# A list scheduler that books VectorE and GpSimd around each other's SBUF reads

## The chip, the cores and the metric

The kernel runs on one core of one Trainium2 chip. The metric is the device time of one execution in microseconds (us), the median of several runs. Before the change it is 1306.06 us, the median of 3 runs that lay between 1305.51 and 1308.34 us.

## What is computed

The reference is one residual block in float32 on 1024 tokens of width 1024. All of it is computed by the kernel:

```
h    = rms_norm(x, norm_w) * (1 + scale(c)) + shift(c)
proj = h @ W_in               # q, k, v, z of mixer A; q, k, v, z of mixer B; two gates; beta, decay
A    : causal conv + SiLU on q, k, v; l2 norm of q, k; gated delta rule, 8 heads of 128
y_A  = (headwise rms_norm(A) * silu(z_A)) @ P_A
B    : causal window attention, 12 heads of 64, in 3 groups with dilations 1, 4, 16
y_B  = (o_B * softmax over the groups' log denominators * silu(z_B)) @ P_B
x    = x + gate(c) * ((sigmoid(g_A) * y_A + sigmoid(g_B) * y_B) @ W_o)
out  = rms_norm(x, final_norm_w)
```

## The kernel before, in words

**The products.** Activations lie transposed, as 8 tiles of 128 features by 1024 tokens. A float32 product is made of three TensorE products of rounded halves (`hi*hi`, `hi*lo`, `lo*hi`), each 128 by 512 at most. There are 4548 such products (with the projections' names `pj<-big,wh` and `pj<-wh,big` for most of them), and they are the bulk of TensorE's work. ScalarE rounds each weight tile to its `hi` half and GpSimd subtracts to get the `lo` half (`w_split`, L579; tiles `wr` in, `wh` out). The late projections are computed two at a time with Strassen's scheme (`pair`, L674): `w_combine` (L609) forms sums of weight blocks on GpSimd and VectorE (`sums`, L637; tile `ss`), and `pair_out` (L711) adds the seven products up on VectorE out of PSUM into tiles `mid`; a PSUM tile `pj` comes free when its last addition has read it.

**The small chains.** Beside the projections run many chains of small steps that go from TensorE to VectorE or ScalarE and back. `conv` (L855) filters a projection with three VectorE instructions. `n_stream` and `q_stream` (L1217, L1340) multiply a head's k with k and with q and scale the result. `inv_stream` (L1243) inverts 32 by 32 triangles for four heads with 62 VectorE instructions in a row (`mid<-big` and `big<-big,mid`), first for heads 0 to 3 (`inv0`), then for 4 to 7 (`inv1`). `merge_stream` (L1271) assembles each head's inverse by small products with evacuations between them, `rec_stream` (L1430) runs a head's 8 chunks of the delta rule, three products one after the other per chunk. `attn_unit` (L1531) is one piece of attention, `combine` (L1636) the weights of the three groups (tile `fga`). Between these, `part` (L821) rounds stored sums of h (named T1 to T4): it is issued as soon as its load is, so its ScalarE copy `big<-mid` can stand in ScalarE's queue before the load has landed.

**The planner.** The order of all engines is made by a list scheduler in the kernel's own Python code. Every chain is a generator (`Stream`), with a priority. `Sched.run` (L240) lets the chain of best priority go whose next step is due by the planner's own clock of TensorE, `clk["pe"]`; the big projections (`projections`, priority 99) fill what is left. Each instruction that is issued passes through `Sched.book` (L137), which adds a length to the clock of its engine and so settles when the chain is due again. The lengths are a table of formulas in ns: n elements per partition on VectorE cost n/0.96 + 150, a GpSimd `tensor_tensor` costs 2.2 n + 400. An engine's queue runs strictly in the order so made; on the chip nothing is reordered. So where a step takes longer than booked, TensorE reaches the step that needs it early, and stands.

Names in the profile: `L110` is the wrapper that issues nearly every instruction, so groups are told apart by tiles: `big` 128x1024 work tiles, `mid` 128x512, `pj` and `sb` PSUM tiles, `sq` 128x128, `TT` and `Xb` the inverses, `dnw` a norm weight.

Of the kernel before, what the change touches and what calls it, by code (L numbers as in the profile page):

```python
# [34 lines left out]
LO_POOL = ("A11", "S3")  # L35
WORKERS = 2
NMID = 6
BLK1 = "k1 k3 q0 q1"
NW = 8

# [4 lines left out]
def _free(ap):  # L45
    n = 1
    for s in list(ap.shape)[1:]:
        n *= s
    return n


class Event:
# [64 lines left out]
class Sched:  # L117


    def __init__(self, nc):  # L120
        self.clk = dict(pe=600.0, act=600.0, dve=600.0, pool=600.0, dma=600.0)
        self.streams = []
        self.cur = None
        self.pe = Engine(self, nc.tensor, "pe")
        self.act = Engine(self, nc.scalar, "act")
        self.dve = Engine(self, nc.vector, "dve")
        self.pool = Engine(self, nc.gpsimd, "pool")
        self.sp = Engine(self, nc.sync, "dma")
        self.table = None

    def now(self):
        return self.clk["pe"]
# [3 lines left out]

    def book(self, e, op, out, a, k):  # L137
        n = _free(a[1] if op == "tensor_reduce" else out)
        done = self.cur.done
        others = max([t for q, t in done.items() if q != e], default=0.0)  # L140
        start = max(self.clk[e], self.clk["pe"], others)
        if e == "pe":
            start = self.clk["pe"]
            if op == "transpose":
                c = 109
            else:
                r = k.get("rhs", a[2] if len(a) > 2 else None)
                if r.dtype == F32R:
                    c = n / 2.4 + 13.4
                elif r.shape[0] <= 64:  # L150
                    c = 30 if out.shape[0] == 32 else 60 if out.shape[0] == 64 else n / 1.1
                else:
                    c = n / 0.6 + 9 if n > 8 else 60
            end = start + c
            self.clk["pe"] = end
            hop = 190
        elif e == "dma":
            b = n * 4 * out.shape[0] * (2 if out.shape[-1] < P else 1)
            end = max(self.clk[e] + max(470, b / 360), max(self.clk["pe"], others) + 1500 + b / 360)
            self.clk[e] = end  # L160
            hop = 950
        else:
            if e == "act":
                c = n / 1.2 + (385 if "accum_out" in k else 195)
                if not isinstance(k.get("bias", 0.0), float) and "accum_out" not in k:
                    c += 160
                f = TABLE.get(k.get("func", a[2] if len(a) > 2 else None))
                if f and f != self.table:
                    self.table = f
                    c += 1280  # L170
            elif e == "dve":
                c = n / 0.96 + 150
                if op == "tensor_scalar":
                    c = n / 1.92 + 215
                elif op == "scalar_tensor_tensor" and n > 8:
                    c += 60
                elif op == "reciprocal":
                    c = n * 6.2 + 70
            else:
                c = n * 2.2 + 400 if op == "tensor_tensor" else n * 1.27  # L180
                if k.get("op") == OP.pow:
                    c = n * 165 + 300
                elif n == 8 * P and k.get("op") == OP.mult:
                    c = 1900
            end = start + c
            self.clk[e] = end
            hop = 130
        done[e] = end + hop
        self.cur.last = max(self.cur.last, end + hop)
# [79 lines left out]
def hybrid_block_kernel(ctx: ExitStack, tc: tile.TileContext, x, c, norm_w, ada_w, ada_b, w_tiles, w_vb0, w_vb1,  # L269
# [3 lines left out]
    pe, act, dve, pool, sp = S.pe, S.act, S.dve, S.pool, S.sp  # L273
# [305 lines left out]
    def w_split():  # L579
# [15 lines left out]
        for u in units[FIRST:]:  # L595
            if hasattr(u, "srcs"):
                yield from w_combine(u)
                continue
            yield u.raw_ev
            u.hi = yield from wh.get(F32R, shape=[P, u.n])  # L600
            u.lo = yield from wh.get(F32R, shape=[P, u.n])
            act.activation(u.hi, u.raw, AF.Copy)
            yield
            pool.tensor_tensor(u.lo, u.raw, u.hi.bitcast(F32), op=OP.subtract)
            wr.put()
            S.set(u.ev)
            yield S.now()

    def w_combine(u):  # L609
# [26 lines left out]

        def sums():  # L637
            yield u.raw_ev[1]
            pool.tensor_tensor(s1, a21, a22, op=OP.add)
            dve.tensor_tensor(s2, s1, a11, op=OP.subtract)  # L640
            S.set(ev_s2)
            yield ev_s2
            pool.tensor_tensor(a21, a11, a21, op=OP.subtract)
            S.set(ev_s3)
            yield u.ev["A12"]
            pool.tensor_tensor(a11, a12, s2, op=OP.subtract)
            S.set(ev_s4)

        ss = yield from spare.get()
        s2, s1 = ss[:, 0:half], ss[:, half:2 * half]  # L650
        ev_s2, ev_s3, ev_s4 = Event(), Event(), Event()
        yield lambda: u.raws
        a11, a12 = u.raws[0][:, 0:half], u.raws[0][:, half:]
# [1395 lines left out]
```

## Time and profile before

| what | us |
|---|---|
| median of 3 runs | 1306.06 |
| the profiled execution's own time | 1307.42 |
| its span, first to last instruction | 1305.7 |
| PE (TensorE) busy | 1228.0 |
| DVE (VectorE) busy | 825.0 |
| ACT (ScalarE) busy | 565.7 |
| POOL (GpSimd) busy | 484.1 |

The mean granted TensorE clock is 0.977 of full speed. In the chain of waits and in the instruction rows, the square brackets hold the idle time just before an instruction and what ended it. A row of the table by stages gives, for a stretch of time, the busy time of each engine, the granted clock and the DMA share.

### The profile page before, as it was taken

The page shows a single profiled execution, that of the slowest core. Times are in us where ns is not written, and L with a number is a line of the kernel's source. Part 1 is how long each engine was busy: PE and PEld are TensorE (multiplying, and loading weights), DVE is VectorE, ACT ScalarE, POOL GpSimd, SP SyncE. Part 2 cuts the span into 40 slices and gives each one's busy share as a digit, 9 for nine tenths or more (in the row PEclk, how much of TensorE's full clock was granted, in tenths as well). Part 3 has the DMA queues.
Part 4 walks back from the last instruction along what each step waited for, and adds up shares of the span by engine and source line. Part 5 has one row for each costly group of instructions (what it writes and reads, how often), then busy time and mean ns, then how long its engine had stood idle before and what let it go on. Part 6 is the DMA issues. An engine that isn't in the chain of part 4 may idle for free. (4 is left out here: it accounts for less than half of the span.)

```text
span 1305.7 us, 19690 instructions
## 1 busy us (share of the span) xinstructions
PE 1228.0 (94%) x7111; PEld 1012.7 (78%) x7111; DVE 825.0 (63%) x1477; ACT 565.7 (43%) x1176; POOL 484.1 (37%) x274
## 2 busy tenths in 40 slices
PE   5799999997977999999899999999989999999997
PEld 3598888876967888877688778877777788888886
DVE  6667798999675655546655865466465557365433
ACT  5547544553242435455533436773542341122211
POOL 4632834642031543432424343245234422123400
PEclk9899999998978999999899999999999999999999
DMA  9464566872854465547785576457445498343422
GB/s 357 145 203 155 153 202 200 260 230 71 253 173 154 134 200 160 149 122 223 247 255 181 167 214 188 127 163 245 144 119 161 130 313 279 120 155 124 144 97 82
DMA packets 166739, 234.99 MB, mean 180 GB/s; under 512 B 42953, under 2 KB 107633, under 8 KB 166642
## 3 DMA queue, kind: packets, MB, share of 16 engines
q1 hardware_dynamic: 166498, 233.47, 56.3%
q8 instruction: 56, 0.92, 0.3%
q14 instruction: 41, 0.34, 0.1%
q10 hardware_dynamic: 144, 0.26, 0.1%
HBM read 154.86 MB, written 78.83 MB: 179 GB/s over the span
## 5 line engine op out<-in xcount | busy, mean ns | idle before, releaser
L110 PE MATMUL pj<-big,wh 128*128 128x512 f32 x3468 | 869.2, 401 | 17.3 <-POOL big L110 8.1
L110 PEld LDWEIGHTS pj<-big,wh 128*128 128x128 f32 x3468 | 636.8, 190 | 156.2 <-POOL big L110 10.1
L110 POOL TENSOR_TENSOR wh<-wr,wh 128x1024 fp32r<-128x1024 f32 (+4 forms) x92 | 215.6, 2344 | 427.0 <-ACT wh L110 357.9
L110 ACT ACTIVATE wh<-wr 128x1024 fp32r<-128x1024 f32 (+4 forms) x119 | 109.9, 924 | 186.9 <-PE pj L110 109.8
L110 DVE TENSOR_TENSOR mid<-mid,pj 128x512 f32<-128x512 f32 x150 | 106.3, 722 | 87.4 <-PE pj L110 70.4
L110 ACT ACTIVATE big<-big 128x1024 f32<-128x1024 f32 (+1 forms) x61 | 64.6, 1059 | 136.9 <-DVE big L110 115.4
L110 PE MATMUL pj<-wh,big 128*128 128x256 f32 (+2 forms) x702 | 112.3, 316 | 3.7 <-DVE big L110 1.1
L110 PEld LDWEIGHTS pj<-wh,big 128*128 128x128 f32 x702 | 100.2, 199 | 10.1 <-POOL wh L110 1.6
L110 POOL TENSOR_TENSOR ss<-wr 128x512 f32<-128x512 f32 x23 | 29.7, 1292 | 152.3 <-DMA wr<-in_w_tiles_dram 130.9
L110 PEld LDWEIGHTS sb<-sq,big 128*128 128x128 f32 x464 | 68.6, 198 | 16.3 <-ACT sq L110 7.5
L110 PE MATMUL sb<-sq,big 128*128 128x128 f32 x464 | 73.6, 285 | 7.4 <-ACT sq L110 6.6
L110 DVE TENSOR_TENSOR big<-big,big 128x1024 f32<-128x1024 f32 (+3 forms) x40 | 63.4, 1585 | 23.5 <-ACT big L110 21.4
L110 DVE SCALAR_TENSOR_TENSOR big<-pj,cw,big 128x1023 f32<-128x1023 f32 (+2 forms) x54 | 69.0, 1278 | 4.5 <-ACT big L110 3.2
L110 ACT ACT_TABLE_LOAD x47 | 60.3, 1283 | 5.9 <-DVE big L110 2.9
L110 POOL TENSOR_TENSOR big<-mid,big 128x512 fp32r<-128x512 f32 x24 | 37.4, 1570 | 56.8 <-ACT big L110 42.0
L110 ACT ACTIVATE mid<-sb 128x384 f32<-128x384 f32 (+5 forms) x75 | 34.3, 459 | 49.5 <-PE sb L110 48.3
L110 ACT ACTIVATE mid<-mid 128x512 f32<-128x512 f32 (+1 forms) x63 | 38.4, 611 | 28.4 <-DVE mid L110 27.9
L110 DVE TENSOR_TENSOR big<-mid,big 128x512 fp32r<-128x512 f32 (+1 forms) x36 | 34.7, 982 | 24.1 <-ACT big L110 18.4
L110 PE MATMUL pj<-big,big 128*128 128x512 f32 x210 | 49.1, 389 | 0.0
L110 ACT ACTIVATE mid<-mid,sta 128x128 f32<-128x128 f32 (+1 forms) x96 | 42.2, 441 | 14.3 <-DVE sta L110 14.1
L110 ACT ACTIVATE big<-sb,gsm 128x128 f32<-128x128 f32 x56 | 20.4, 366 | 62.4 <-DVE sq L110 62.4
L110 PE MATMUL sb<-big 128*128 128x128 f32 (+2 forms) x320 | 40.3, 322 | 7.1 <-DVE big L110 4.5
(140 smaller groups left out, 1488.8 us busy)
## 6 DMA issues: line engine op xcount, KB each, us to landing
wr<-in_w_tiles_dram SPq DMA_DIRECT2D x64, 512.0 KB, 4.3
rkd<-big SPq DMA_DIRECT2D x32, 512.0 KB, 5.0
big<-rkd SPq DMA_DIRECT2D x64, 256.0 KB, 3.5
big<-in_ada_w_dram SPq DMA_DIRECT2D x24, 512.0 KB, 9.0
big<-in_x_dram SPq DMA_DIRECT2D x16, 512.0 KB, 5.1
gd<-mid SPq DMA_DIRECT2D x32, 256.0 KB, 3.2
big<-gd SPq DMA_DIRECT2D x16, 512.0 KB, 4.7
zd<-mid SPq DMA_DIRECT2D x28, 256.0 KB, 3.2
```

Of the source, the lines that this page charges most:

```text
L110: r = f(*a, **k)
```

## The change

Three things change in `book`, all of them numbers and bookkeeping inside the planner, and only once the planner's TensorE clock has passed 60 us (`6e4` ns). A GpSimd `tensor_tensor` is booked at 2.2 n + 150 instead of 2.2 n + 400. Every GpSimd instruction, and every VectorE instruction with two or more tensor inputs that all lie in SBUF, is now moved in the plan behind any booked instruction of the other engine with which it would overlap (`shared`). The stretches so booked are kept in `held`, the last 40 of each engine. VectorE instructions with an input in PSUM, or with one tensor input, are booked as before. The two new settings `SUMS = "ppp"` and `W_LO = "p"` choose the engine of four instructions; with these values they stay on GpSimd, where they were. No instruction is added or removed, save that ScalarE's table of functions is loaded 45 times instead of 47. The order on all engines changes from the planner's 60 us on.

```
+        self.held = dict(dve=[], pool=[])
+    def shared(self, e, start, c):
+        for a, b in sorted(self.held["pool" if e == "dve" else "dve"]):
+            if a < start + c and start < b:
+                start = b
+        return start
...
-                c = n * 2.2 + 400 if op == "tensor_tensor" else n * 1.27
+                c = n * 2.2 + (150 if self.clk["pe"] > 6e4 else 400) if op == "tensor_tensor" else n * 1.27
...
+            if e != "act" and self.clk["pe"] > 6e4:
+                ins = [a[q] for q in dict(scalar_tensor_tensor=(1, 3), tensor_scalar=(1, 1), memset=()).get(op, (1, 2)) if q < len(a)]
+                if e == "pool" or len(ins) > 1 and all(_in_sbuf(q) for q in ins):
+                    start = self.shared(e, start, c)
+                    self.held[e] = self.held[e][-40:] + [(start, start + c)]
             end = start + c
```

What the new order is, at three places on which the prediction rests. In the rows below, `L110` (before) and `L116` (after) are the same wrapper.

The first place is TensorE's queue at the k-with-k products of head 7 (`n_stream`), before the change. `sb66` and `sb67` are the PSUM tiles of its two halves, and the `pj` rows are projection products, two to a row.

```order
L110 MATMUL pj23_2793<-big46_478,wh44_2540 128x512 x2
L110 MATMUL sb66_2840<-big117_2421 128x128 x4
L110 MATMUL pj23_2793<-big50_516,wh43_2539 128x512 x2
L110 MATMUL sb67_2853<-big117_2421 128x128 x4
L110 MATMUL pj23_2793<-big51_517,wh43_2539 128x512 x2
```

The same place after the change, from the first half to the second:

```order
L116 MATMUL sb66_2826<-big118_2444 128x128 x4
L116 MATMUL pj23_2767<-big46_478,wh44_2537 128x512 x2
L116 MATMUL pj23_2767<-big50_516,wh43_2536 128x512 x2
L116 MATMUL pj23_2767<-big51_517,wh43_2536 128x512 x2
L116 MATMUL pj23_2767<-big50_516,wh44_2537 128x512 x2
L116 MATMUL pj23_2767<-big54_543,wh43_2536 128x512 x2
L116 MATMUL pj23_2767<-big55_544,wh43_2536 128x512 x2
L116 MATMUL pj23_2767<-big54_543,wh44_2537 128x512 x2
L116 MATMUL pj23_2767<-big58_580,wh43_2536 128x512 x2
L116 MATMUL pj23_2767<-big59_581,wh43_2536 128x512 x2
L116 MATMUL pj23_2767<-big58_580,wh44_2537 128x512 x2
L116 MATMUL pj23_2767<-big60_615,wh43_2536 128x512 x2
L116 MATMUL sb67_2876<-big118_2444 128x128 x4
```

Two products stood between the halves, and now 22 do. A little ahead of this place, head 4's k-with-q products stood 44 products behind the end of head 4's q projection and now stand 66 behind it. Further on, the first merge product stood behind 1284 projection products of the whole and now stands behind 1344; between it and the merge's second step stood 18 products, and now 6. Near the end, head 7's recurrence (`rec_stream`) stood between products 2952 and 3129 and now stands between 2709 and 2892; at one place there three of its steps follow each other with no projection product between. The three groups' `combine` products stood at 3135 to 3153 and now stand at 3228 to 3237, of 4548; the last stage's products (with `w_pa`) begin at 3468 in both.

The second place is ScalarE's queue at the merges of heads 0 and 1, before the change. `big<-mid` rows are the copies of T2 to T4 that wait for a load, the rows with 32x256, 32x8x32 or 64x512 are the merges' evacuations, and `sq<-sb` is the first of a recurrence.

```order
L110 ACTIVATE big138_3154<-mid75_3276 128x512
L110 ACTIVATE big142_3292<-mid76_3293 128x512
L110 ACTIVATE mid77_3331<-sb77_3307 32x256 x2
...
L110 ACTIVATE TT1_104<-sb82_3488 32x8x32 x2
L110 ACTIVATE big144_3531<-mid84_3532 128x512
L110 ACTIVATE big145_3567<-mid85_3568 128x512
L110 ACTIVATE big146_3570<-mid86_3571 128x512
L110 ACTIVATE wh57_3582<-wr29_3476 128x512
L110 ACTIVATE big147_3573<-mid87_3591 128x512
L110 ACTIVATE mid88_3602<-sb84_3558 64x512
L110 ACTIVATE sq3_3609<-sb85_3606 128x128
```

The same place after the change:

```order
L116 ACTIVATE mid79_3376<-pj28_3294 128x512
L116 ACTIVATE mid80_3397<-sb76_3379 32x256 x2
...
L116 ACTIVATE big141_3479<-mid84_3510 128x512
L116 ACTIVATE wh57_3522<-wr29_3405 128x512
L116 ACTIVATE TT1_104<-sb80_3485 32x8x32 x2
...
L116 ACTIVATE big144_3577<-mid86_3578 128x512
L116 ACTIVATE qss_242<-sb82_3547 128x8
L116 ACTIVATE mid87_3588<-sb84_3567 64x512
L116 ACTIVATE big145_3591<-mid88_3592 128x512
L116 ACTIVATE big146_3594<-mid89_3595 128x512
L116 ACTIVATE big147_3597<-mid90_3617 128x512
L116 ACTIVATE sq3_3623<-sb86_3620 128x128
```

The first merge's evacuation no longer stands right behind two such copies. Other copies moved: one now stands ahead of merge 1's second evacuation, where none stood; one instead of four ahead of its third; and three instead of none right ahead of the first recurrence's `sq<-sb`. On VectorE, merge 1's last evacuation stands behind six instructions of `inv1` in both orders.

The third place is VectorE's queue in the fourth pair of projections from the end, before the change. Rows with `pj` are `pair_out`'s additions, and the row with `dnw` is the end of head 7's recurrence.

```order
L110 TENSOR_TENSOR wh202_9243<-ss21_9160,wh201_9242 128x1024
L110 TENSOR_TENSOR mid244_9201<-mid244_9201,pj123_9222 128x512
L110 SCALAR_TENSOR_TENSOR big230_9226<-big231_9227,dnw_90,big230_9226 128x8x32 x4
L110 TENSOR_TENSOR mid242_9128<-mid242_9128,pj124_9249 128x512
L110 TENSOR_TENSOR mid247_9311<-mid246_9291,pj126_9290 128x512
```

The same pair's last addition after the change, with what stands ahead of it:

```order
L116 TENSOR_TENSOR fga0_109<-mid242_9171 128x8x4
L116 TENSOR_TENSOR mid243_9173<-mid243_9173 128x32
L116 TENSOR_TENSOR fga1_110<-mid243_9173 128x8x4
L116 TENSOR_TENSOR mid243_9173<-mid243_9173,fga1_110 128x32
L116 RECIPROCAL mid243_9173<-mid243_9173 128x32
L116 TENSOR_TENSOR fga1_110<-mid243_9173 128x8x4
L116 TENSOR_TENSOR mid239_9090<-mid239_9090,pj128_9208 128x512
L116 TENSOR_TENSOR mid244_9178<-mid244_9178 128x32
```

The end of head 7's recurrence has left this place; the small instructions of two groups' `combine` have come in its stead.

More of the change, by code (lines that the diff above doesn't have):

```diff
@@ L37 @@
 NMID = 6
+SUMS = "ppp"
+W_LO = "p"
 BLK1 = "k1 k3 q0 q1"
@@ L49, in _free, with _in_sbuf @@
     return n
+def _in_sbuf(ap):
+    return getattr(ap, "space", PSUM) != PSUM
 class Event:
@@ L603, in w_split @@
             yield
-            pool.tensor_tensor(u.lo, u.raw, u.hi.bitcast(F32), op=OP.subtract)
+            dict(d=dve, p=pool)[W_LO].tensor_tensor(u.lo, u.raw, u.hi.bitcast(F32), op=OP.subtract)
             wr.put()
@@ L638, in sums @@
             yield u.raw_ev[1]
-            pool.tensor_tensor(s1, a21, a22, op=OP.add)
+            SUM[0].tensor_tensor(s1, a21, a22, op=OP.add)
             dve.tensor_tensor(s2, s1, a11, op=OP.subtract)
@@ L642, in sums @@
             yield ev_s2
-            pool.tensor_tensor(a21, a11, a21, op=OP.subtract)
+            SUM[1].tensor_tensor(a21, a11, a21, op=OP.subtract)
             S.set(ev_s3)
             yield u.ev["A12"]
-            pool.tensor_tensor(a11, a12, s2, op=OP.subtract)
+            SUM[2].tensor_tensor(a11, a12, s2, op=OP.subtract)
             S.set(ev_s4)
+        SUM = [dict(d=dve, p=pool)[e_] for e_ in SUMS]
         ss = yield from spare.get()
```

## The prediction

> **What bounds the kernel now.** The page comes first, for the span and the engine that fills it.
>
> ```profile
> span 1305.7 us, 19690 instructions
> PE 1228.0 (94%) x7111; PEld 1012.7 (78%) x7111; DVE 825.0 (63%) x1477; ACT 565.7 (43%) x1176; POOL 484.1 (37%) x274
> ```
>
> TensorE is busy 94% of the span, and the change adds and removes no product, so it can only act on the time in which TensorE stands or runs slowly. Where that lies, the table by stages says (columns: stretch, PE, PEld, DVE, ACT, POOL busy, granted clock, DMA share, GB/s).
>
> ```profile
> 75.00:280.00 205.00, 205.00 (x1101) 174.60 (x1101) 170.63 (x299) 109.07 (x219) 95.80 (x47) 1.00 0.65 203
> 280.00:440.00 160.00, 135.72 (x1038) 123.35 (x1037) 120.67 (x253) 62.33 (x134) 47.78 (x29) 0.89 0.51 158
> 440.00:1012.00 572.00, 550.75 (x3481) 441.60 (x3480) 333.07 (x706) 278.48 (x665) 221.06 (x121) 0.99 0.59 180
> 1012.00:1286.00 274.00, 273.40 (x1201) 224.53 (x1200) 140.44 (x120) 67.94 (x86) 73.81 (x40) 1.00 0.51 168
> 160.00:330.00 170.00, 161.61 (x843) 134.91 (x842) 160.47 (x288) 78.36 (x139) 73.57 (x37) 0.98 0.62 195
> ```
>
> TensorE never stands from 75 to 280 us and hardly from 1012 to 1286. From 280 to 440 it stands 160.00 - 135.72 = 24.3 us, from 440 to 1012 it stands 572.00 - 550.75 = 21.3 us. The last row adds that VectorE is 160.47/170 = 94% busy just ahead of the first of these: there it is the engine that sets the pace. What ended the waits is read from the timeline, TensorE's rows alone (start, length, what, in brackets the idle time before and who ended it).
>
> ```profile
> 299.39 1.16 PE L110 MATMUL sb<-big,big 128*128 128x128 f32 x8 [3.22 <-ACT big L110]
> 313.66 2.08 PE L110 MATMUL sb<-big 128*128 128x128 f32 x8 [4.47 <-DVE big L110]
> 365.93 0.26 PE L110 MATMUL sb<-TT,mid 32*32 32x32 f32 x1 [4.80 <-ACT mid L110]
> 389.08 1.21 PE L110 MATMUL sb<-TT,mid 64*64 64x64 f32 x16 [1.76 <-ACT mid L110]
> 393.71 0.80 PE L110 MATMUL sb<-big,TT 128*128 128x128 f32 x2 [2.26 <-DVE TT L110]
> 418.37 2.08 PE L110 MATMUL sb<-sq,big 128*128 128x128 f32 x8 [5.02 <-ACT sq L110]
> 635.09 1.43 PE L110 MATMUL sb<-big 64*128 64x256 f32 x6 [1.61 <-DVE mid L110]
> 652.66 1.22 PE L110 MATMUL sb<-sq,big 128*128 128x128 f32 x4 [1.55 <-ACT sq L110]
> 965.58 0.97 PE L110 MATMUL pj<-big,wh 128*128 128x512 f32 x3 [1.38 <-DVE mid L110]
> 977.09 0.37 PE L110 MATMUL sb<-cst,fga 128*32 128x128 f32 x1 [1.95 <-DVE fga L110]
> ```
>
> The waits cost twice, because the granted clock falls after some of them:
>
> ```profile
> 288.50:311.40 22.90, 17.47 (x96) 14.53 (x94) 22.31 (x34) 10.82 (x19) 12.89 (x7) 1.00 0.32 98
> 311.40:318.30 6.90, 4.64 (x15) 4.06 (x16) 6.62 (x20) 0.00 (x0) 0.16 (x1) 0.51 0.30 81
> 362.70:376.30 13.60, 10.38 (x111) 9.80 (x112) 12.13 (x25) 5.00 (x10) 4.34 (x3) 0.50 0.60 200
> 390.00:396.80 6.80, 4.54 (x22) 4.13 (x21) 6.56 (x12) 1.08 (x4) 3.04 (x3) 0.50 0.46 154
> 417.30:424.10 6.80, 5.73 (x27) 5.73 (x28) 1.10 (x4) 2.37 (x8) 2.50 (x2) 0.50 0.28 93
> 977.10:980.50 3.40, 3.09 (x7) 2.22 (x8) 2.28 (x11) 1.22 (x4) 0.76 (x1) 0.50 0.55 212
> ```
>
> At half clock TensorE worked 4.64 + 10.38 + 4.54 + 5.73 + 3.09 = 28.4 us in the five slow rows; half of it, 14.2 us, is lost. Idle time and lost clock together, 24.3 + 21.3 + 14.2 = 59.8 us, are what an order can win, or add to.
>
> A rule bears on the clock. The first row has the wait of 3.22 us and keeps a clock of 1.00; the wait of 4.47 us is followed by one of 0.51, but so is, at 977, a wait of 1.95 us by one of 0.50. The Trainium skill ("TensorE: Matmul & The Clock Gate", Part 1) says that the clock halves after an idle window of about 3.4 us; by that the slow rows at 390 and 977 would not be there. The trace differs, and the sum goes by the trace.
>
> **What the planner gets wrong.** VectorE's instructions with two SBUF inputs stretch where GpSimd works, and those that read PSUM don't. The end of head 7's recurrence shows it, and so does `inv0` at 307 us.
>
> ```profile
> 996.88 3.78 DVE L110 SCALAR_TENSOR_TENSOR big<-big,dnw,big 128x256 f32<-128x256 f32 x4 [0.73 <-DMA big<-otd]
> 997.84 2.54 POOL L110 TENSOR_TENSOR wh<-wr,wh 128x1024 fp32r<-128x1024 f32 x1 [3.37 <-ACT wh L110]
> 1001.31 0.96 PE L110 MATMUL pj<-big,wh 128*128 128x512 f32 x3 [2.01 <-DVE mid L110]
> 307.15 2.52 POOL L110 TENSOR_TENSOR big<-big,cst 128x1024 f32<-128x1024 f32 x1
> 307.47 2.43 DVE L110 TENSOR_TENSOR mid<-big 128x207 f32<-128x207 f32 x1
> 309.93 1.85 DVE L110 TENSOR_TENSOR big<-big,mid 128x207 f32<-128x207 f32 x1
> 311.82 0.36 DVE L110 TENSOR_TENSOR mid<-big 128x192 f32<-128x192 f32 x1
> L110 DVE SCALAR_TENSOR_TENSOR big<-big,dnw,big x32: 472/479/2625, 601.4 to 998.1; 128x256 f32<-128x256 f32 x32
> L110 DVE SCALAR_TENSOR_TENSOR big<-sb,s_all,big 128x128 f32<-128x128 f32 x128 | 35.3, 341 | 8.3 <-PE sb L110 8.3
> L110 POOL TENSOR_TENSOR wh<-wr,wh x92: 1303/2395/3458, 58.4 to 1224.0; 128x1024 fp32r<-128x1024 f32 x75, 128x768 fp32r<-128x768 f32 x12, 128x816 fp32r<-128x816 f32 x2, 128x512 fp32r<-128x512 f32 x2
> ```
>
> An instruction of 479 ns (the middle of minimum, median and maximum in ns) took up to 2625 ns, about one GpSimd instruction longer, and TensorE's wait of 2.01 us follows. Two instructions of `inv0` took 2.43 and 1.85 us where the next took 0.36 us. The 128 that read PSUM have a mean of 341 ns. The planner before knows nothing of this, and books 2653 ns (2.2 x 1024 + 400) for the GpSimd subtraction whose median is 2395 ns; the changed one books 2403 ns, and the waiting.
>
> **The change part by part.** All durations are those of the profiled execution, whose own time is 1307.42 us, 1.4 us over the median of 1306.06 us. The start, to 60 us of the planner's clock, and the last stage keep their order nearly, so they stay.
>
> *The waits of 3.22 and 4.47 us.* Their steps now stand 22 and 20 products further behind what they wait for. What a product is worth is read from the chain of waits:
>
> ```profile
> 1152.28 134.48 PE pj L110 x592
> ```
>
> 134.48/592 = 0.227 us. So 5.0 and 4.5 us of work come ahead of them, just over the waits: 7.7 us go. With the second goes the slow stretch behind it, 4.64/2 = 2.3 us. The bounds: nothing, if VectorE is late by as much more (its pace rules there); 10.0 us if all goes. I take 10.0, since on VectorE the steps ahead are the same few. What is late next are the merges, and 60 more products (13.6 us) stand ahead of the first of them.
>
> *The wait of 4.80 us* had ScalarE's evacuation behind copies whose loads had not landed:
>
> ```profile
> 417.52 0.63 ACT L110 ACTIVATE big<-mid 128x512 fp32r<-128x512 f32 x1 [6.84 <-DMA mid<-tdT]
> ACT big L110 <- DMA mid<-tdT: 32.0, 8, 9.6
> ```
>
> The second row: eight such waits of ScalarE, 32.0 us in all. These two copies no longer stand there; but 6 products cover the step instead of 18. I take 3.8 of the 4.8 us as gone, and half of the slow stretch's 10.38/2 = 5.2 us, 2.6 us. Bounds: 0 and 10.0 us.
>
> *The waits of 1.76, 2.26 and 5.02 us* I leave as they are. The 2.26 us had merge 1's last evacuation behind six instructions of `inv1`, and it still stands there; the 5.02 us had one copy waiting for its load ahead of a `sq<-sb` (the row at 417.52), and now three stand ahead of another. Bounds: 9.0 us less, or up to the price of the first rival more.
>
> *The waits from 440 to 1012 us.* Four of those shown end with VectorE, where GpSimd overlaps it: 1.61 + 1.38 + 1.95 + 2.01 = 7.0 us, and the slow stretch at 977 adds 3.09/2 = 1.5 us. The recurrence that met GpSimd at 997 us has moved away, but two groups' `combine` now stand at that place, and the wait of 1.95 us was one `combine`'s. I take half, 4.2 us; bounds 0 and 8.5 us. The other waits there, 21.3 - 7.0 = 14.3 us, end mostly with ScalarE or loads; they change places, with no sign that I can read.
>
> *New waits.* The planner, which now counts GpSimd 250 ns cheaper, packs some steps closer. Head 7's recurrence has three steps with no projection product between. The nearest row is the wait of 1.55 us for a `sq<-sb`; twice that, 3.1 us, is my price; bounds 0 and 6 us.
>
> Sum: 10.0 + 3.8 + 2.6 + 4.2 - 3.1 = 17.5 us less. From 1307.4 that is 1289.9 us, and on the footing of the median 1306.1 - 17.5 = 1288.6 us; I say 1289.
>
> The rule behind the booking is weighed once. The row of 3.78 us shows one long instruction of four, and no slow sharing. The Trainium skill ("SBUF — State Buffer", Who interferes with whom) says that a VectorE instruction with two SBUF inputs and a GpSimd instruction that reads SBUF exclude each other for the whole instruction, whichever starts first. By that, booking in plan order still guesses who starts first on the chip, and a wrong guess leaves the wait where it was. Halving the fourth term is my allowance for it; by a rule of slow sharing the same rows would give no 2.6 us instruction at all.
>
> **The rivals.** *Slower: ScalarE's queue stands behind loads.* Three places at the merges of heads 0 and 1 now have such copies ahead of an evacuation that TensorE waits for. Each costs like the row at 418.37: 5.02 us and 5.73/2 = 2.9 us of clock, 7.9 us. One is in the time already. If all three bite while the first term holds, the rest nets to nothing, and the head 7 price falls due, the time is 1306.1 - 10.0 + 2 x 7.9 + 3.1 = 1315 us; with two biting, 1307 us. It decides from the third on. For it: 32.0 us in eight waits. Against it: most of these 32 us don't reach TensorE, which shows two such waits. Chance 0.16.
>
> *No change: VectorE's pace.* It is 94% busy from 160 to 330 us. If it is what the merges really wait for, the waits of 3.22 and 4.47 us only move 50 us on and are paid there, with their clock. Then 4.2 us less and 3.1 us more remain: 1305 us. For it: six of the waits end with VectorE. Against it: from 280 to 440 us it works 120.67 of 160 us, so it waits itself there. Chance 0.11.
>
> *Much faster.* If the plan now fits so well that the waits of 1.76, 2.26 and 5.02 us go too, with their slow stretches (4.54 + 5.73 = 10.3, half of it 5.1 us), 14.2 us more are won: 1274 us; with the whole fourth term 1270 us. Chance 0.08.
>
> That the change doesn't do what it says is excluded: all queues differ from the planner's 60 us on.
>
> **How the numbers follow.** My forecast has 0.65, the rivals 0.16, 0.11 and 0.08. About 0.2% (2.6 us) is what measurements of this kernel can tell from no change. Faster is 0.65 + 0.08 = 0.73, same 0.11, slower 0.16. The range reaches down to the third rival's 1270 us and up to 1311 us, in the first's span between two and three places, which leaves about 0.16 out. The forecast's own range is 1277 to 1302 us.
>
> **What would show it.** Right: TensorE idle from 280 to 440 us under 17 us, no waits over 1 us at the head 4 and head 7 steps, the first merge with 60 more products behind TensorE at about the same time. Wrong: waits of over 4 us at the merges with ScalarE's copies of T3 and T4 behind their loads (first rival), or a longer wait at the first merge for VectorE (second). VectorE's long instructions should remain in number and TensorE's waits behind them fall; if these waits stay too, the booking missed.

## The result, and the profile after

The changed kernel takes 1313.66 us (median of 5 runs, 1309.80 to 1317.71), the kernel before in the same session 1305.51 us (5 runs, 1301.56 to 1308.34). The ratio is 1.0070, with a 95% interval of 1.0047 to 1.0093: slower by 0.7%, where 1.3% faster was forecast, and above the 1311 us up to which the range went. The profiled execution of the changed kernel took 1313.38 us against 1307.42 us before. Two executions of the study, one of the kernel before with 1386 us and one of `lock_only` with 4777 us, took far longer than the others of their kernel and are left out of all ratios.

The page's first rows and then the table by stages, for the changed kernel (columns as in the prediction: stretch, PE, PEld, DVE, ACT, POOL busy, granted clock, DMA share, GB/s):

```profile
span 1311.7 us, 19671 instructions
PE 1230.0 (94%) x7111; PEld 1012.4 (77%) x7111; DVE 819.3 (62%) x1477; ACT 564.5 (43%) x1174; POOL 486.7 (37%) x274
```

```profile
75.00:280.00 205.00, 198.95 (x1066) 169.39 (x1065) 171.48 (x291) 99.23 (x197) 92.59 (x46) 0.98 0.62 194
280.00:440.00 160.00, 143.21 (x1064) 128.93 (x1064) 123.98 (x251) 65.47 (x141) 52.86 (x31) 0.91 0.57 176
440.00:1012.00 572.00, 547.01 (x3484) 437.98 (x3483) 321.36 (x715) 284.99 (x680) 219.83 (x120) 0.99 0.59 178
1012.00:1286.00 274.00, 271.23 (x1190) 222.28 (x1189) 142.28 (x119) 67.76 (x85) 75.98 (x39) 1.00 0.52 167
```

TensorE's idle time against before: 280 to 440 us, 24.3 to 16.8 us, 7.5 us won, where the sum had 7.7 + 3.8 = 11.5 us. But 75 to 280 us, 0 to 6.05 us; 440 to 1012 us, 21.3 to 25.0 us; 1012 to 1286 us, 0.6 to 2.8 us. The span is 6.0 us longer, 1311.7 - 1230.0 = 81.7 us of it idle where it was 1305.7 - 1228.0 = 77.7 us; the other 2.0 us are busy time. So TensorE stands 4.0 us more in all, and the question is which waits came where others went. (The stretches are by time, and the same work lies some us later in the changed kernel.)

The view of TensorE's waits answers it (who waits, for whom, us in total, times, longest). First before, then after:

```profile
PE sb L110 <- ACT mid L110: 12.4, 6, 4.8
PE sb L110 <- DVE big L110: 11.7, 5, 4.5
PE sb L110 <- ACT sq L110: 6.6, 2, 5.0
PE pj L110 <- DVE mid L110: 5.4, 6, 2.0
```

```profile
PE pj L116 <- DVE mid L116: 19.0, 17, 3.1
PE sb L116 <- DVE big L116: 8.9, 6, 2.1
PE pj L116 <- ACT mid L116: 7.1, 1, 7.1
PE pj L116 <- DVE ik L116: 5.1, 1, 5.1
PE sb L116 <- ACT mid L116: 4.0, 3, 3.0
PE sb L116 <- ACT sq L116: 2.2, 3, 1.5
```

An `sb` product is a step of a small chain that waits for the step before it. A `pj` product is a projection product, and in the rows shown it mostly waits for its PSUM tile to come free: for a convolution, for an addition of `pair_out`, for the eviction of a value group (`v_evac`). In other rows it waits for an operand; the largest of these, for GpSimd's `big` in the first 50 us, is 8.1 us before and 7.9 us after. All rows of the view added by these two names: `sb` fell from 48.9 to 23.5 us, 25.4 us won; `pj` rose from 20.3 to 50.0 us, 29.7 us lost. The new order spared the chains and paid mostly with PSUM.

Two of these waits in the timeline (start, length, what, in brackets the idle time before). VectorE and GpSimd near 130 us, and TensorE's product that waits, after the change:

```profile
125.70 6.43 DVE L116 TENSOR_TENSOR_SCAN big<-big,cst 128x128 f32<-128x128 f32 x8
127.08 1.98 POOL L116 TENSOR_TENSOR big<-big,ds_all 128x1024 f32<-128x1024 f32 x1
129.03 2.50 POOL L116 TENSOR_TENSOR wh<-wr,wh 128x1024 fp32r<-128x1024 f32 x1
132.05 3.88 DVE L116 SCALAR_TENSOR_TENSOR big<-pj,cw,big 128x1023 f32<-128x1023 f32 x3
136.08 2.47 PE L116 MATMUL pj<-big,wh 128*128 128x512 f32 x5 [5.12 <-DVE ik L116]
```

The same two steps before the change:

```profile
123.53 3.88 DVE L110 SCALAR_TENSOR_TENSOR big<-pj,cw,big 128x1023 f32<-128x1023 f32 x3
127.33 2.63 DVE L110 TENSOR_TENSOR_SCAN big<-big,cst 128x128 f32<-128x128 f32 x8
```

Before, head 3's convolution, which empties a `pj` tile, goes ahead of head 1's eight scans; after, behind them. The scans take 6.43 us instead of 2.63 us, since two GpSimd instructions lie across them, and the convolution starts only behind them. The name `ik` in the bracket is only the VectorE instruction that ends nearest to the tile's release: the convolution's third instruction ends at 132.05 + 3.88 = 135.93 us, and the product starts at 136.08 us.

ScalarE near 366 us, after the change:

```profile
366.69 0.63 ACT L116 ACTIVATE big<-mid 128x512 fp32r<-128x512 f32 x1 [11.09 <-DMA mid<-tdT]
367.23 1.06 ACT L116 ACTIVATE mid<-pj 128x512 f32<-128x512 f32 x2
367.86 1.43 PE L116 MATMUL pj<-wh,big 128*128 128x256 f32 x5 [7.10 <-ACT mid L116]
```

A copy of T3 stands 11.09 us for its load, behind it two evictions of value groups, and TensorE stands 7.10 us for the first of them.

### The profile page after: what moved, and what is told of

The parts are those of the page before. It is cut to its first block, busy times and chain, and to the rows that moved or that the text cites. A ratio compares the mean times of both kernels' runs of the same rounds, so it can differ in the third digit from the quotient of the medians.

```text
span 1311.7 us, 19671 instructions
## 1 busy us (share of the span) xinstructions
PE 1230.0 (94%) x7111; PEld 1012.4 (77%) x7111; DVE 819.3 (62%) x1477; ACT 564.5 (43%) x1174; POOL 486.7 (37%) x274
## 5 line engine op out<-in xcount | busy, mean ns | idle before, releaser
L116 PE MATMUL pj<-big,wh 128*128 128x512 f32 x3504 | 884.4, 402 | 38.6 <-DVE mid L116 19.0
L116 PEld LDWEIGHTS pj<-big,wh 128*128 128x128 f32 x3504 | 644.9, 191 | 181.7 <-DVE mid L116 20.8
L116 POOL TENSOR_TENSOR wh<-wr,wh 128x1024 fp32r<-128x1024 f32 (+4 forms) x92 | 217.7, 2368 | 433.1 <-ACT wh L116 303.4
L116 ACT ACTIVATE wh<-wr 128x1024 fp32r<-128x1024 f32 (+4 forms) x119 | 109.8, 923 | 159.0 <-PE pj L116 119.0
L116 DVE TENSOR_TENSOR mid<-mid,pj 128x512 f32<-128x512 f32 x152 | 107.9, 722 | 73.5 <-PE pj L116 67.4
L116 ACT ACTIVATE big<-big 128x1024 f32<-128x1024 f32 (+1 forms) x61 | 64.6, 1059 | 153.4 <-DVE big L116 132.1
L116 PE MATMUL pj<-wh,big 128*128 128x256 f32 (+2 forms) x702 | 111.2, 316 | 12.2 <-ACT mid L116 7.1
L116 PEld LDWEIGHTS pj<-wh,big 128*128 128x128 f32 x702 | 100.0, 200 | 19.1 <-ACT mid L116 7.3
L116 PEld LDWEIGHTS sb<-sq,big 128*128 128x128 f32 x464 | 67.2, 194 | 14.4 <-ACT sq L116 3.3
L116 PE MATMUL sb<-sq,big 128*128 128x128 f32 x464 | 72.4, 281 | 3.6 <-ACT sq L116 2.2
L116 POOL TENSOR_TENSOR ss<-wr 128x512 f32<-128x512 f32 x23 | 29.8, 1295 | 121.3 <-DMA wr<-in_w_tiles_dram 117.0
L116 DVE TENSOR_TENSOR big<-big,big 128x1024 f32<-128x1024 f32 (+3 forms) x40 | 60.8, 1525 | 21.2 <-ACT big L116 19.1
L116 DVE SCALAR_TENSOR_TENSOR big<-pj,cw,big 128x1023 f32<-128x1023 f32 (+2 forms) x54 | 68.9, 1277 | 3.7 <-ACT big L116 2.4
L116 POOL TENSOR_TENSOR big<-mid,big 128x512 fp32r<-128x512 f32 x24 | 37.7, 1581 | 51.0 <-ACT big L116 32.7
L116 ACT ACTIVATE mid<-sb 128x384 f32<-128x384 f32 (+5 forms) x75 | 34.5, 459 | 43.9 <-PE sb L116 43.2
L116 ACT ACTIVATE big<-sb,gsm 128x128 f32<-128x128 f32 x56 | 20.4, 366 | 71.9 <-DVE sq L116 71.7
L116 DVE TENSOR_TENSOR big<-mid,big 128x512 fp32r<-128x512 f32 (+1 forms) x36 | 39.0, 1105 | 18.0 <-ACT big L116 12.7
L116 PE MATMUL pj<-big,big 128*128 128x512 f32 x210 | 49.1, 389 | 0.0
L116 ACT ACTIVATE mid<-mid,sta 128x128 f32<-128x128 f32 (+1 forms) x96 | 42.2, 440 | 15.9 <-DVE sta L116 11.1
L116 ACT ACTIVATE mid<-mid 128x512 f32<-128x512 f32 (+1 forms) x63 | 38.1, 610 | 23.5 <-DVE mid L116 18.4
L116 DVE SCALAR_TENSOR_TENSOR big<-big,pj 128x1024 f32<-128x1024 f32 x16 | 19.5, 1220 | 42.6 <-PE pj L116 42.6
```

The lines of the kernel that those rows point to most:

```text
L116: r = f(*a, **k)
```

## The theories

**A**: booking the two engines apart puts VectorE's evictions off, and so TensorE is late. **B**: the cheaper GpSimd price packs steps too closely. **C**: neither has a sign of its own. Any change of the plan's numbers makes a new order; a new order meets other waits of a few us, which the plan doesn't know (stretched VectorE instructions, copies behind loads), and the order of before has few.

The results of all runs that compute the whole block, with the medians of each. `pj` and `sb` are the sums of the rows of the view of waits, as above. Ratios are to the kernel before in the same session (medians 1304.2 to 1305.6 us).

| kernel | us | ratio, 95% interval | pj | sb | pj + sb |
|---|---|---|---|---|---|
| before | 1305.5 | | 20.3 | 48.9 | 69.2 |
| after | 1313.7 | 1.0047 to 1.0093 | 50.0 | 23.5 | 73.5 |
| cost_only | 1326.7 | 1.0153 to 1.0202 | 34.4 | 52.2 | 86.6 |
| lock_only | 1345.3 | 1.0271 to 1.0335 | 49.1 | 45.8 | 94.9 |
| price370_before | 1319.4 | 1.0060 to 1.0138 | 50.0 | 26.4 | 76.4 |
| price450_before | 1315.6 | 1.0053 to 1.0111 | 41.8 | 37.3 | 79.1 |
| price140_after | 1314.2 | 1.0042 to 1.0088 | 48.7 | 27.7 | 76.4 |
| price180_after | 1319.8 | 1.0087 to 1.0157 | 48.8 | 27.9 | 76.7 |
| evict_before | 1323.2 | 1.0114 to 1.0182 | 46.4 | 33.8 | 80.2 |
| evict_after | 1339.4 | 1.0240 to 1.0307 | 55.2 | 37.0 | 92.2 |
| after_load | 1305.5 | 0.9984 to 1.0024 | 47.8 | 20.7 | 68.5 |
| hold_scans | 1308.6 | 1.0010 to 1.0045 | 43.1 | 24.7 | 67.8 |
| hold_copies | 1310.9 | 1.0032 to 1.0083 | 51.4 | 21.8 | 73.2 |
| hold_adds | 1310.8 | 1.0029 to 1.0066 | 44.4 | 27.3 | 71.7 |
| hold_all | 1303.6 | 0.9974 to 1.0012 | 40.8 | 23.9 | 64.7 |
| hold_more | 1293.7 | 0.9892 to 0.9947 | 24.8 | 31.8 | 56.6 |

Neither column of waits goes with the time alone: `after_load` has 47.8 us of `pj` waits and is level with before. Their sum goes with it nearly: 56.6 us in the fastest kernel, 94.9 us in the slowest.

## Experiments 1 and 2: the two halves of the change

`cost_only` takes the booking out (`if e != "act" and self.clk["pe"] > 1e9:`), `lock_only` the price (`400` for the pair of 150 and 400).

> Only the planner's price of a GpSimd tensor_tensor falls from 400 to 150 ns over its slope (from 60 us on); nothing is booked apart. Theory A (booking apart makes TensorE late: VectorE's additions and convolutions, which free PSUM, are put off behind two-SBUF instructions): about as before, 1303 to 1308 us. Theory B (the cheaper price packs steps too closely): all of the loss, 1312 to 1315 us. Theory C (neither has a sign of its own; each new order falls well or badly by its own coincidences of some us): anything from 1299 to 1315 us, and the differences of the two halves from before do not add up to the whole change's 8 us.

> Only the booking apart; GpSimd keeps its price of 400 ns. Theory A: all of the loss or more, 1312 to 1318 us. Theory B: as before or faster, 1298 to 1307 us. Theory C: anything from 1299 to 1315 us, with waits for PSUM tiles at places that neither before nor the changed kernel has.

The price alone costs 22 us, the booking alone 40 us, both together 8 us. A needed the price alone near the kernel before, B the booking alone; neither is. The halves don't add up, as C had it, but 1327 and 1345 us lie beyond C's 1315 too: new orders can cost more than I had thought.

## Experiments 3 and 4: the same orders without the exclusion

These two kernels leave out GpSimd's subtractions: in the place of each stand two instructions that fill its output with zeros and read nothing. The order is that of before (`nolock_before`) or of the changed kernel (`nolock_after`).

```
-            r = f(*a, **k)
+            if self._n == "pool" and op == "tensor_tensor" and k["op"] == OP.subtract:
+                self._e.memset(a[0].bitcast(F32), 0.0)
+                r = self._e.memset(a[0].bitcast(F32), 0.0)
+            else:
+                r = f(*a, **k)
```

> The order of before, to the instruction, but each GpSimd subtraction is two memsets of its output (the result is wrong: GpSimd's subtractions are left out). If memsets do not hold VectorE up, VectorE's excess of about 129 us over its undisturbed durations falls below 50 us. Theory A and C, in which the order decides: the time falls by some us, since 8 to 15 us of TensorE's waits end with stretched VectorE instructions: 1291 to 1299 us. If the exclusion hardly reaches TensorE: 1302 to 1306 us.

> The order of the changed kernel with the same replacement (GpSimd's subtractions are left out). If the loss comes through stretched VectorE instructions that free PSUM tiles too late (the exclusion itself, met at worse places), it vanishes: within 3 us of the order of before with the replacement. If the loss is in the order alone (additions behind other work, copies behind loads), it stays: 5 to 9 us over it, with the wait of about 7 us near 362 us still there.

The order of before then takes 1264.48 us (ratio 0.9697, 0.9674 to 0.9720), that of the changed kernel 1273.94 us (0.9762, 0.9735 to 0.9788). The first lies far below every range on record for it: I had put the exclusion's price at 15 us at most. The page's row of the order of before with the memsets:

```profile
PE 1212.2 (96%) x7111; PEld 1006.2 (80%) x7111; DVE 712.6 (56%) x1477; ACT 566.3 (45%) x1176; POOL 394.3 (31%) x441
```

With the same 1477 instructions VectorE is busy 712.6 us instead of 825.0 us: 112.4 us of its time went with GpSimd's subtractions. It is not that GpSimd works less. In that trace 139 of VectorE's instructions with two SBUF inputs overlap a memset alone, and together they are 0.8 us longer than undisturbed ones (the shortest tenth of the same instruction and shape in four traces); before, 165 overlap a GpSimd instruction that reads SBUF, and they are 125 us longer. The Trainium skill ("SBUF — State Buffer", Who interferes with whom) says that a VectorE instruction with two SBUF inputs contends with a GpSimd instruction that reads SBUF and not with one that only writes it; these runs agree. Not all of the 40 us are the exclusion's: 13.5 us are won before the 144th projection product, where also, I take it, a memset needn't wait for what the subtraction reads.

Of the 112.4 us the change took 825.0 - 819.3 = 5.7 us. And the orders differ by 9.5 us without the subtractions too (I had expected 5 to 9 us for a loss in the order alone), against 8 us with them. So the loss is in the order, which both A and C allow. The exclusion only makes its waits larger on both sides: without it the new order loses 12.5 us at `pj` (10.8 to 23.3 us) instead of 29.7, and wins 6.6 us at `sb` (31.8 to 25.2 us) instead of 25.4. In the changed order without the subtractions the long wait for ScalarE is still there, at the same product, the 1297th:

```profile
PE pj L120 <- DVE mid L120: 9.5, 10, 2.8
PE pj L120 <- ACT mid L120: 6.2, 1, 6.2
```

## Experiments 5 to 8: a small step in one price

`n * 2.2 + 400` becomes `n * 2.2 + (370 if self.clk["pe"] > 6e4 else 400)`, or 450, in the kernel before; 150 becomes 140 or 180 in the changed one.

> The kernel before, with one number of the plan moved a little: from 60 us on GpSimd's tensor_tensor is priced with 370 ns over its slope instead of 400 (1% of a large one). No booking apart. It moves about as many instructions as the change itself. Theory A or B (the change costs by what it books): so small a price does nothing of its own, 1303 to 1308 us. Theory C (the time of an order is set by local coincidences that any new plan draws anew, and the order of before is a good draw): 1310 to 1345 us.

> The same with 450 ns instead of 400. Theory A or B: 1302 to 1308 us. Theory C: again 1310 to 1345 us, and another value than with 370 ns, by waits at other places.

> The changed kernel with 140 ns instead of 150 in the same price (under 0.5% of a large one). Theory A or B: within 3 us of the changed kernel, 1310 to 1317 us. Theory C: anything from 1300 to 1345 us.

> The changed kernel with 180 ns instead of 150. Theory A or B: within 3 us of the changed kernel, 1310 to 1317 us. Theory C: anything from 1300 to 1345 us.

Without any booking apart, 30 ns less on GpSimd's price cost the kernel before 14 us, and 50 ns more cost it 10 us: 1319.4 and 1315.6 us. That is as much as the whole change, and by waits of the same kind. `price370_before`, waits of TensorE:

```profile
PE pj L110 <- DVE mid L110: 21.6, 12, 5.6
PE pj L110 <- DVE big L110: 12.6, 4, 4.8
```

With 140 instead of 150 ns the changed kernel keeps its time (1314.2 us), with 180 it loses 6 us. A and B said 1302 to 1308 us for the first pair and 1310 to 1317 us for the second, and fall. C holds: the ten orders that the planner made anew in this study (the rows from after to after_load), with booking and without, all have 34 to 55 us of `pj` waits, and the kernel before has 20.3 us. Most win a part of that back at `sb`; with both together nine of the ten stand longer than before. What the change costs, by this reading, is the loss of an order with few `pj` waits; the next experiments test it.

## Experiments 9 to 12: single instructions put later in the changed order

If C is right, the loss can be undone by hand at the places where it arises. The plan stays as the change makes it; only the issue of single instructions is held back until another one, further on in the plan, has been issued.

```
+HOLD = {822: 855, ..., 2618: 2619, 2840: 2859, ...}   # instruction: issue it behind this one
+            if i in HOLD:
+                s.kept.append((HOLD[i], f, a, k))
...
+            for q in [q for q in s.kept if q[0] == i]:
+                q[1](*q[2], **q[3])
```

> The changed kernel's plan, with nine instructions put later in their engines' queues: head 1's eight scans on VectorE and the Exp behind them on ScalarE go behind the three instructions of head 3's k convolution. If the wait of 5.12 us near 136 us is the convolution standing behind the scans, it goes, with the slow clock behind it (6.8 us at half clock, 3.4 us): product 480 comes 6 to 8 us sooner. Theory C, with waits that add up along TensorE: 1305 to 1309 us in the end. If a later wait swallows it (something other than TensorE sets the pace): 1311 to 1314 us.

> The changed kernel's plan, with two copies put later in ScalarE's queue: that of T3 block 1 behind the first eviction of value group 1, that of T3 block 3 behind head 0's merge copy. If the waits of 7.10 and 2.95 us are ScalarE standing behind their loads, they go to under 2 us together, and the time falls to 1304 to 1309 us; if the next copies behind loads take their place, 1311 to 1314 us.

> The changed kernel's plan, with seven VectorE instructions that have two SBUF inputs put behind the next addition of a pair's output, which frees a PSUM tile. If the waits between 600 and 1010 us are additions behind instructions that GpSimd stretches, some 8 to 10 us of the 25 us of TensorE's idle time from 440 to 1012 us go: 1302 to 1307 us. If the additions are late for another reason (their inputs): 1311 to 1314 us.

> All three edits, 18 instructions put later. If the three gains add up: 1290 to 1298 us, below the kernel before. If they hide one another: 1300 to 1308 us. If the waits only move: 1310 to 1314 us.

`hold_scans` at the place of the 5.12 us:

```profile
123.71 3.92 DVE L123 SCALAR_TENSOR_TENSOR big<-pj,cw,big 128x1023 f32<-128x1023 f32 x3 [1.32 <-ACT big L123]
125.54 2.41 POOL L123 TENSOR_TENSOR wh<-wr,wh 128x1024 fp32r<-128x1024 f32 x1
127.54 2.90 DVE L126 TENSOR_TENSOR_SCAN big<-big,cst 128x128 f32<-128x128 f32 x8
```

The convolution runs beside GpSimd's instruction at its full speed, since it reads PSUM; the scans come behind it, and the wait is gone. Between the 288th and the 576th projection product, counted in the two traces, TensorE needs 77.0 us instead of 83.8 us: 6.8 us won, as expected, and 5.1 us in the end. `hold_copies` wins 2.7 us, not clear of noise (its interval overlaps that of the changed kernel): the 7.10 us go, but the next copy behind its load takes part of their place, through a weight tile, and a wait of 2.13 us for GpSimd's half of that tile follows:

```profile
369.12 0.63 ACT L123 ACTIVATE big<-mid 128x512 fp32r<-128x512 f32 x1 [3.49 <-DMA mid<-tdT]
369.66 1.56 ACT L123 ACTIVATE wh<-wr 128x768 fp32r<-128x768 f32 x2
370.54 0.58 PE L123 MATMUL pj<-wh,big 128*128 128x256 f32 x1 [3.56 <-ACT wh L123]
```

`hold_adds` wins 2.9 us of the 8 to 10 us expected, not clear of noise either. One addition shows why. Before the edit it stood behind a subtraction of 3.39 us, and TensorE stood 3.14 us (the changed kernel):

```profile
665.75 3.13 POOL L116 TENSOR_TENSOR wh<-wr,wh 128x1024 fp32r<-128x1024 f32 x1 [2.82 <-ACT wh L116]
666.57 3.39 DVE L116 TENSOR_TENSOR wh<-ss,wh 128x1024 fp32r<-128x1024 f32 x1
669.88 0.67 DVE L116 TENSOR_TENSOR mid<-mid,pj 128x512 f32<-128x512 f32 x1
670.61 2.34 PE L116 MATMUL pj<-big,wh 128*128 128x512 f32 x9 [3.14 <-DVE mid L116]
```

In `hold_adds` the subtraction stands behind the addition. But the late convolution ahead of both, three instructions from SBUF alone, starts 1.9 us earlier (660.53 us instead of 662.47), and GpSimd's instruction 4.4 us earlier, since ScalarE's copy that releases it had stood 3.04 us for TensorE and now doesn't wait. So GpSimd now falls on the convolution, which takes 6.57 us instead of 4.17 us:

```profile
660.53 6.57 DVE L123 SCALAR_TENSOR_TENSOR big<-big,cw,big 128x1023 f32<-128x1023 f32 x3
661.35 3.36 POOL L123 TENSOR_TENSOR wh<-wr,wh 128x1024 fp32r<-128x1024 f32 x1
667.02 0.68 DVE L123 TENSOR_TENSOR mid<-mid,pj 128x512 f32<-128x512 f32 x1
667.76 2.50 PE L123 MATMUL pj<-big,wh 128*128 128x512 f32 x5 [4.00 <-DVE mid L123]
```

The wait is now 4.00 us. All three edits together, `hold_all`, take 1303.6 us, 10.1 us less than the changed kernel: the three gains (5.1 + 2.7 + 2.9 = 10.7, each known to some 3 us) are in keeping with adding up. The 1290 to 1298 us that I had put on record for that were missed, because two of the gains are smaller than I had expected. With 18 instructions put later the changed kernel is level with before.

## Experiments 13 to 16: what was still open

`hold_more` holds seven instructions more, the late convolution of the last rows among them. `evict_before` and `evict_after` rank the streams that free PSUM first in the planner (0.5 instead of 10 for `finish` and `v_evac`, and of 2.5 for `pair_out`). `after_load` is the changed kernel in which the plan waits for a T block's load before its copy is issued:

```
+    S.add(part(name, i, m, t[:, HALVES[0]], t[:, HALVES[1]], at=S.cur_last()), 1.5, f"{name}{i}")
...
     def part(name, i, src, hi, lo, evs=(), at=None):
-        yield
+        yield at
```

> All of hold_all, and seven instructions more put later: head 6's late convolution behind the addition that came to stand behind it (a wait of 3.99 us at 658 us), the T3 block 2 copy and its subtraction behind the third eviction of value group 1 (3.36 and 1.95 us), a GpSimd sum behind the A11 subtraction that TensorE waits for (2.84 us), one subtraction behind an addition near 985 us (1.37 us). If waits for evictions add up along TensorE: 8 to 11 us less than hold_all's 1303.6 us, 1292 to 1296 us, below the kernel before. If new waits take their place again: 1300 to 1304 us.

> The kernel before, with the streams that free PSUM (convolutions, evictions of value groups, the pairs' additions) ranked first in the planner instead of last or in the middle; no booking apart. If late evictions are what a new draw of the order costs: the waits of pj products on VectorE and ScalarE stay under 10 us, and the time is below the other new draws' 1313 to 1345 us, 1290 to 1308 us. If the rank does not matter or only moves the lateness to the chains: 1310 to 1330 us.

> The same ranks in the changed kernel. If the booking itself does something good once evictions come first: below evict_before, 1280 to 1300 us. If it does nothing of its own: within 8 us of evict_before, with either sign. If it does harm: more than 8 us above it.

> The changed kernel, in which the plan issues a copy of a T block to ScalarE only when its load has landed by the plan's clock; the order changes from 335 us on. If copies behind loads are a loss of the plan: ScalarE's eight waits for these loads shrink from about 30 to under 10 us, the wait of 7.10 us goes, and the time is 1300 to 1308 us. If the draw of the order outweighs it: 1310 to 1330 us, with those waits gone all the same.

`hold_more` takes 1293.7 us, 20 us under the changed kernel and 0.8% under the kernel before: the best of the study. Its 1292 to 1296 us were on record for waits that add up along TensorE. It doesn't show that the change pays: these instructions were picked in the changed kernel's traces, and no run gives the kernel before the same care. The long waits for VectorE's additions are gone from its view of waits:

```profile
PE pj L123 <- DVE mid L123: 7.5, 14, 1.3
```

The evictions' rank is not the cause: with it first, the sum of `pj` waits is 46.4 and 55.2 us, no smaller than in the other new orders, and the times are 1323.2 and 1339.4 us. I take it that the evictions are on time in the plan anyway and late on the chip alone, behind instructions that take longer than planned; no run shows the plan's side of this. `evict_before`:

```profile
PE pj L110 <- DVE mid L110: 22.6, 13, 4.3
PE pj L110 <- DVE big L110: 9.3, 3, 5.6
```

`evict_after` lies 16 us above `evict_before`, beyond the 8 us of "nothing of its own". But a step of 10 to 50 ns moves an order by up to 14 us, so I read no harm of the booking into one pair.

`after_load` does what it says. ScalarE's waits for these loads, first in the changed kernel and then in `after_load`:

```profile
ACT big L116 <- DMA mid<-tdT: 26.1, 4, 11.1
```

```profile
ACT big L116 <- DMA mid<-tdT: 7.4, 6, 3.6
```

TensorE's wait of 7.10 us is gone too. In its place stands one of 4.49 us for another eviction on ScalarE, 48 products earlier, with no load ahead of it: there ScalarE waits for VectorE. The time is 1305.5 us, level with before. How much of the 8 us is the rule and how much the luck of a new order, one run can't tell.

## Why the prediction was wrong

The step that failed is the price of new waits: 3.1 us, from one place, for an order that is new on every engine from the planner's 60 us on. The runs show 29.7 us more of `pj` waits, which outweigh the 25.4 us won at the chains. Term by term:

**The waits of 3.22 and 4.47 us** (10.0 us with the slow clock): right in mechanism. From 137 to 335 us, where both steps lie, TensorE has no wait over 1 us. Between the 1008th and the 1152nd projection product, which hold both, it needs 44.7 us instead of 54.2 us: 9.5 us. That this comes so near to 10.0 is partly luck. Some 2 us of it are small products that now stand elsewhere (80 in the stretch instead of 96), and 2.50 us are paid back at its end: there TensorE waits for VectorE's convolution, at 337.81 us, with half clock behind it, where before it waited 1.08 us. To the 1200th product 7.2 us are left. So a little of the second rival, VectorE's pace, is in it.

**The wait of 4.80 us** (6.4 us): the wait is gone, but its mechanism is not. The copies of T3 stand ahead of other evictions now, and cost 7.10 and 2.95 us there; in `hold_copies` both are gone, and 3.56 and 2.13 us have come. The slower rival had this mechanism, at the merges; it bit once at a merge and once at an eviction into `mid`, of which I hadn't thought. Alone it wouldn't have turned the sign: the idle time from 280 to 440 us is 16.8 us, under the 17 us that were to show the forecast right. But it is so by luck, since the 5.02 and 2.26 us that I had left as they were went too.

**"The start and the last stage keep their order nearly, so they stay", and TensorE that "never stands from 75 to 280 us"**: this failed at the earliest place. The order changes from the planner's 60 us on, and a stage without a wait can only lose by a new order. It lost 6.05 us, 5.12 us of them at one convolution; `hold_scans` shows it.

**The fourth term** (4.2 us won from 440 to 1012 us) failed in sign: 3.7 us lost. VectorE's long instructions even became fewer there: those more than 0.5 us over their undisturbed length fell from 29 to 19, and its busy time from 333.07 to 321.36 us (over the whole, 96 to 90 and 5.7 us less). But TensorE's waits did not fall with them: those for the additions that free PSUM rose from 5.4 to 19.0 us over the whole, and the two groups' `combine` cost 1.39 us twice where one had cost 1.95 us. The sentence that other waits "change places, with no sign that I can read" hid this: the waits that a new order brings have a sign, since the kernel before had few of them. "Halving" the term for wrong guesses was far from enough.

**New waits** (3.1 us, at head 7's recurrence): found there, about as priced. At 873 to 876 us, behind the 2760th product, three steps without a projection product between wait 0.91, 0.44 and 0.59 us, 1.9 us in all. But the other new waits, which the term didn't have, are ten times its size, 29.7 us of `pj` waits.

**The clock.** The prediction's slow stretches leave out two, 635.8 to 639.2 and 649.4 to 656.2 us: 8.65 us of work at half clock, 4.3 us lost, so that 59.8 us should be some 64 us. And its puzzle, a wait of 3.22 us that keeps the clock and one of 1.95 us that doesn't, has an answer in the trace, given in the last section.

So the waits of chains that I could see went, and more of them than I had counted: chains win 25.4 us. What failed is the sum itself. It counted the waits that the trace of before shows, and for those of the new order it had one price, from one place. The two halves and the small steps show the true price of a new order here: 8 to 40 us over the kernel before with no care taken for evictions or loads. Why the kernel before has so few `pj` waits the runs don't show; nor do they show whether booking apart is worth anything on the mean over many orders. Without it the four new orders took 1316 to 1327 us, with it the others 1305 to 1345 us.

## What to carry to other kernels

Where an instruction order is made by a planner, cost a change of the planner as a new draw and not as an edit: the waits that go can be read in the trace, those that come can't, and an order that already has few of them mostly loses: here nine of ten new orders were slower than the one before, and one was level. Test that cheaply, by a step of 1% in a number of no importance: if it moves the time as much as the change does, the change's own sign can't be read from one run. Then repair the new order where it waits. Along an engine that is 94% busy such repairs came through nearly in full here: with 8.8 us less of `pj` and `sb` waits `hold_all` is 10.1 us faster than the changed kernel, with 16.9 us less `hold_more` is 20 us faster.

## What the runs showed of the hardware that I had not expected

GpSimd's subtractions cost VectorE 112.4 of its 825.0 us in this kernel, and two memsets in the place of each don't. The cost is not spread: eight scans take 6.43 us instead of 2.63, and three instructions of a convolution from SBUF take 6.57 us where three of a convolution from PSUM take 3.92 us, both with GpSimd at work beside them. And moving one instruction can bring another of VectorE's under one of GpSimd's, so that a release comes later, not sooner: a wait of 4.00 us for one of 3.14 us.

TensorE's clock was halved after idle time well under 3.4 us. All changes of the granted clock in the traces before and after lie a whole number of 3.41 us steps apart. Cut into such windows from 60 us to the last 30 us, both traces together have 14 full-clock windows behind which the clock was halved, with 1.61 to 3.41 us of idle time in the window; in those behind which it stayed full it is 1.74 us at most. So in these two traces it is about half a window that counts, wherever the gaps lie in it. (Six more traces of the study agree, but for two windows with 0.95 and 1.14 us behind which the clock was halved.) The wait of 1.95 us at 977 us lay within one window; that of 3.22 us at 299 us lay across two, with 1.69 and 1.52 us, and kept the clock.
